# Three moves in the order of work: first loads on a second queue, chains that end in the next stage, vectors put behind a norm

## The chip, the cores and the metric

The kernel runs on one core of a Trainium2 chip. The core has a matrix engine (TensorE, PE in the profile; its weight loads are PEld), VectorE (DVE), ScalarE (ACT), GpSimd (POOL), SyncE (SP, which here only issues DMAs), and 16 DMA engines. The metric is the device time of one execution in microseconds (us). Three timed runs of the kernel before gave 2895.5, 2902.23 and 2908.86 us; the median is 2902.23 us.

## What is computed

The input is a sequence `x` of 512 rows by 1024 columns and a context of 256 rows. All is float32. Cut to what matters:

```
first_block:
  mod = silu(c) @ w_ada + b_ada                 # six vectors of 1024, likewise from c_ctx
  h   = rms_norm(x, gain) * (1 + scale) + shift # and the same for ctx
  q, k, v, gates of 4 retention and 4 mLSTM heads = h @ w_in
  retention and mLSTM scans, forward and backward, started from the context's states
  x += g1 * ((sig(.)*(y_ret @ w_ret_up) + sig(.)*(y_ml @ w_ml_up)) @ w_out)
  x += g2 * swiglu(norm(x));  x = rms_norm(x, final_gain)
second_block, four layers (latent attention, sliding window, long convolution, latent attention):
  mx = silu(c_2) @ w_mod[layer] + b_mod[layer]  # three vectors of 1024, likewise from c_ctx_2
  hx = rmsnorm(x, g_pre) * (1 + scale) + shift  # and the same for ctx
  x += gate * rmsnorm(mixer(hx, hc), g_post)
```

## The kernel before, in words

**Products.** Activations lie with features on partitions, `x` as 8 tiles of 128x512, the context as 8 of 128x256. A float32 matrix is split into a high and a low part (`split`, L398 on ScalarE and L399 on VectorE), and a product is three matmuls per 128 rows of weights (`mac`, L442 to L444). A weight tile is loaded by SP into one of 4 buffers `raw` (`wload`, L404), split, and used.

**Order.** The code is written as Python generators; each `yield` ends a step. `weave((g, n), (h, m), ...)` always takes the next step of the generator that is furthest behind its number n, and so merges them; a generator with more steps than its number goes on alone at the end. `islice(g, n)` hands over n steps, `chain` puts generators one behind another. The order so written is a priority: a planner walks it with modelled durations, takes for each engine the earliest-written instruction that is ready and whose tile is free, and fixes each engine's order from that. Each engine then runs its list in order. Tiles come from pools: `big` has 53 buffers of 128x512 (tag b), `tmp` 10, `P` 8, the PSUM pools 4 banks and 2 pairs of banks.

**Start** (`first_block`, from L604). SP issues in this order: the constants (L294), 8 small rows of vectors (`rows`, L340), 8 small loads of the filter network (`filter_setup`, L1827 to L1838), 8 loads of `x` and 4 of the context (`load_T`, L485, 256 KB each), then the modulation weights. `load_T` transposes what landed (L491), squares are summed (L232, L236), and `norm1` scales (L571 to L577).

**Vectors.** `mod_stream` makes 18 vectors, 6 of `w_ada` and 12 of `w_mod`; each takes 4 steps (`mod`), each step 2 loads of 512 KB and 16 narrow matmuls (L505), gathered on VectorE (L508, L510) and transposed at the end (L514). `self.mods(n)` weaves in n steps; `need(i)` runs the stream until vector i is there.

**First block's heads.** `dense(pair, ml)` has 12 steps (ND): two for keys, one for the context's keys, two for values, one for the context's values, two for states `S` (L839, L840), and four for queries and gates. `ret_chain(pair)` has 20 steps, 10 for each of 2 heads, and is woven by the number NR = 16; `ml_chain(pair)` has 34 (NM), 17 a head: 4 for the queries, 8 for the four key blocks, 2 for denominators (L1010 to L1015), 2 that spread them and scale (`over_columns` L1386, L1019, L1020), and 1 for the sum (L1024, L1025). Each stage weaves the dense work of one pair with the chain of the pair before and 4 vector steps; the fifth weaves 10 gate products (`bgate`) with the last chain. Chains take their tiles from `tmp` and `P`, dense steps from `big`.

**First latent layer.** `norm3(1)`, the last norm of the first block for the second half of the sequence, is kept as `self.pending` and runs inside the layer's first 41 steps (`stream_tiles`, `lead`): 24 of the norm woven with 6 of products on what is ready, then 8 and 3 steps for the second half. 22 steps with 11 weight tiles follow. In `mla` (L1549) the whole is woven as `(tiles, 30)` with `self.mods(12)`. The fourth layer calls the same code when the stream has nothing left; there the pending norm is `rest` of the third layer.

Of the kernel before, what the change touches and what calls it, by code (L numbers as in the profile page):

```python
# [19 lines left out]
N = 512  # L20
NC = 256
# [10 lines left out]
NR = 16  # L32
NM = 34
# [5 lines left out]
ND = 12  # L39
NM1 = 34  # L40
# [36 lines left out]
WB = 3  # L77
# [115 lines left out]
def weave(*items):  # L193
    for _ in mix(*items):
        pass
# [8 lines left out]
def chain(*gens):  # L204
    for g in gens:
        yield from g
# [49 lines left out]
class Kern:  # L256
# [347 lines left out]
    def first_block(self):  # L604
        nc, I = self.nc, self.I
        st = ExitStack()
        c1 = mp = self.pool("c1", 1, st=st)
        C, X = self.actf(KT, NC), self.actf(KT, N)
        first = self.rows(False, nc.sync)
        next(first)  # L610
        setup = self.filter_setup()
        next(setup)
        inputs = [self.load_T(I["x"][0], N, X), self.load_T(I["ctx"][0], NC, C)]
        for g in inputs:
            next(g)
        self.second_setup()
        late = self.rows(True, nc.gpsimd)
        next(late)
# [286 lines left out]
        def ret_chain(pair):  # L905
            o = out[pair, False]
            for u in range(2):
                h = 2 * pair + u

                strips = [self.P(), self.P()]  # L910
                dist = self.t(), self.t()
                of = self.coff["first"]["dist"][0]
                for z in range(2):
                    nc.sync.dma_start(dist[z], I["k_first"][:, of + 384 * z:of + 384 * z + 512])
                nc.vector.tensor_scalar(strips[0][:, 0:384], dist[0][:, 0:384], lg[:, 4 + h:5 + h], -1.0, ALU.mult, ALU.mult)
                nc.vector.tensor_scalar(strips[1][:, 128:512], dist[1][:, 128:512], lg[:, h:h + 1], None, ALU.mult)
                tmp = self.t(128)
                m0, m1 = strips[0][:, 384:512], strips[1][:, 0:128]
                nc.vector.tensor_scalar(tmp, dist[1][:, 0:128], 0.0, lg[:, 4 + h:5 + h], ALU.min, ALU.mult)
                nc.vector.tensor_scalar(m0, dist[1][:, 0:128], 0.0, lg[:, h:h + 1], ALU.max, ALU.mult)  # L920
                nc.vector.tensor_tensor(m0, m0, tmp, ALU.subtract)
                nc.scalar.activation(strips[0], strips[0], AF.Exp)
                nc.scalar.activation(strips[1][:, 128:512], strips[1][:, 128:512], AF.Exp)
                nc.vector.tensor_tensor(m0, m0, self.ident, ALU.add)
                nc.vector.tensor_copy(m1, m0)
                yield
                S = yield from scores(o.K[u], o.q[u])
                acc = self.mm()
                for d in range(2):
                    qd = HL(self.P(dt=F32R), self.P(dt=F32R))  # L930
                    g = self.t()
                    nc.scalar.activation(g, cf["tpos"] if d == 0 else cf["tpos"][:, ::-1], AF.Exp, scale=lg[:, 4 * d + h:4 * d + h + 1])
                    nc.vector.tensor_tensor(g, g, o.q32[u], ALU.mult)
                    self.split(qd, g)
                    self.mac(acc, [(o.S[u][d], qd)], start=d == 0, stop=False)
                    (finish if d else roots)()
                    yield
                for i in range(4):
                    P = self.t()
                    a = 384 - 128 * i  # L940
                    n0 = 512 - a
                    nc.vector.tensor_tensor(P[:, 0:n0], S[i][:, 0:n0], strips[0][:, a:512], ALU.mult)
                    if n0 < 512:
                        nc.vector.tensor_tensor(P[:, n0:512], S[i][:, n0:512], strips[1][:, 128:128 + 512 - n0], ALU.mult)
                    Ph = HL(self.t(dt=F32R), self.t(dt=F32R))
                    self.split(Ph, P)
                    self.mac(acc, [(o.V[i][:, 128 * u:128 * u + 128], Ph)], start=False, stop=i == 3)
                    yield
                o32 = self.t()
                nc.scalar.copy(o32, acc)  # L950
                nc.vector.tensor_tensor(o.g[u], o.g[u], o32, ALU.mult)
                tail.append((self.rstd1(o32, 4), o.g[u], o.g[u]))
                yret32[h] = o.g[u]
                yield
# [77 lines left out]
        def bgate(k):  # L1032
            for off in (4112, 5136):
                t = sg[k, off] = self.b()
                nc.scalar.activation(t, self.proj(self.wm(W, 0, KT, off + 128 * k), hx, N), AF.Tanh, scale=0.5)
                yield

        weave((dense(0, False), ND), (chain(idle(GD), gates()), 10 + GD), (units, UC))
        weave((dense(1, False), ND), (ret_chain(0), NR), self.mods(4))
        weave((dense(0, True), ND), (ret_chain(1), NR), self.mods(4))  # L1040
        weave((dense(1, True), ND), (ml_chain(0), NM), self.mods(4))
        nbg = 5
        weave((chain(*(bgate(k) for k in range(nbg))), 2 * nbg), (ml_chain(1), NM1), self.mods(4))
        yret, yml = self.acts(4, N), self.acts(4, N)
        for k in range(4):
            self.split(yret[k], yret32[k])
# [32 lines left out]
        w1, s1 = [], [b, b, b, P, P, None, None, None]  # L1079
        weave((merge(), 22), self.mods(4), (chain(idle(PA), self.ahead(I["w_out"][0], 0, KT, s1, w1)), PA + PE0 + PZ))  # L1080
        X = self.actf(KT, N)
# [83 lines left out]
        w2, s2 = [], [b, P, P, P, P, None, None, None]  # L1165
# [308 lines left out]
    def mla(self, j, ctx_out, bg, end):  # L1474
        nc, I = self.nc, self.I
# [60 lines left out]
        def tiles(cs, lag, last=False):  # L1536
            for _ in self.stream_tiles([(load(c), use(c, 0), use(c, 1) if ctx_out or c in (4, 5, 6) else None) for c in cs], lag):
                for x in list(due):
                    if x[0]:
                        x[0] -= 1  # L1540
                    elif next(x[1], None) is None:
                        due.remove(x)
                yield
            while due and last:
                for x in list(due):
                    if next(x[1], None) is None:
                        due.remove(x)

        weave((tiles(order, WB - 2, True), 30), bg)  # L1549

        H = {}

# [265 lines left out]
        return chain(attend(units[-LT:]), stageB(*units[-1])), 10 * LT + 5  # L1818


    def filter_setup(self):

        nc, I = self.nc, self.I
        cp = self.c2
        sm = cp.tile([64, 8], F32, name="fsm")
        w1 = cp.tile([33, 64], F32, name="fw1")
        nc.sync.dma_start(w1, I["c_f_w1_2"][0])  # L1827
        zs = []
        for n, kz in ((N, "k_fz"), (NC, "k_fzc")):
            z = self.t(n)[0:33, :]  # L1830
            nc.sync.dma_start(z, I[kz])
            zs.append(z)
        for i, nm in enumerate(("c_f_b1_2", "c_f_b2_2", "c_f_freq_2")):
            nc.sync.dma_start(sm[:, i:i + 1], I[nm].rearrange("a (f o) -> (a f) o", o=1))
        w2 = cp.tile([64, 64], F32, name="fw2")
        nc.sync.dma_start(w2, I["c_f_w2_2"][0])
        self.ftc = cp.tile([128, 6], F32, name="ftc")
        nc.sync.dma_start(self.ftc, I["k_ftime"])  # L1838
        yield
        for i in range(2):  # L1840
            nc.vector.tensor_tensor(sm[:, 3 + i:4 + i], sm[:, i:i + 1], sm[:, 2:3], ALU.mult)
        self.fh = []

        def sine(ps, n, b):
            arg, r = self.t(n)[0:64, :], self.t(n)[0:64, :]
            nc.scalar.activation(arg, ps, AF.Identity, scale=sm[:, 2:3], bias=b)
            nc.vector.tensor_scalar(r, arg, float(1 / (2 * math.pi)), MAGIC, ALU.mult, ALU.add)
            nc.vector.tensor_scalar(r, r, -MAGIC, None, ALU.add)
            nc.vector.scalar_tensor_tensor(arg, r, -TP1, arg, ALU.mult, ALU.add)
            nc.vector.scalar_tensor_tensor(arg, r, -TP2, arg, ALU.mult, ALU.add)  # L1850
            nc.vector.tensor_scalar(arg, arg, 3.1415925, -3.1415925, ALU.min, ALU.max)
            nc.scalar.activation(arg, arg, AF.Sin)
            return arg

        for z, n in zip(zs, (N, NC)):
            ps = self.mm()
            nc.tensor.matmul(ps[0:64, :n], w1, z, start=True, stop=True)
            h = sine(ps[0:64, :n], n, sm[:, 3:4])
            yield
            ps = self.mm()  # L1860
            nc.tensor.matmul(ps[0:64, :n], w2, h, start=True, stop=True)
            h = sine(ps[0:64, :n], n, sm[:, 4:5])
            f = self.b(dt=F32R)[:, :n]
            nc.scalar.copy(f[0:64, :], h)
            nc.vector.tensor_tensor(f[64:128, :], h, f[0:64, :].bitcast(F32), ALU.subtract)
            self.fh.append(f)
            yield
# [284 lines left out]
```

## Time and profile before

| | before |
|---|---|
| timed runs, median | 2902.23 us |
| profiled execution, its own time | 2904.86 us |
| its span, first to last instruction | 2903.1 us |
| PE busy | 2771.4 us, 95% |
| DVE, ACT, POOL busy | 1800.1, 1321.4, 131.7 us |
| mean granted TensorE clock | 0.981 |
| DMA | 318.95 MB, 110 GB/s over the span |

All times of the trace count from the first instruction of the profiled execution. Busy is time in which an engine ran an instruction; the share of the whole says little of a stage, so the rows further down are of stretches. A wait names what ended it. The granted clock is 1.00 at TensorE's upper level (2.4 GHz) and 0.50 at the lower (1.2 GHz).

### The profile page before, as it was taken

To read this page: it belongs to the slowest core of one execution; us is meant where nothing else is said; L and a number is where in the kernel's file an instruction comes from. 1 tells how busy PE (TensorE), PEld (TensorE's weight loads), DVE (VectorE), ACT (ScalarE), POOL (GpSimd) and SP (SyncE) were. 2 spreads that over 40 slices of the span, in tenths; PEclk is the share of its full clock that TensorE was granted. 3 is DMA by queue.
4 is the path that set the end of the run, shared out by engine and by line. 5 is a ranking of instruction groups with operands and counts; after the bars stand their busy time and mean duration, and the time that the engine had idled before them with its cause. 6 is when DMAs were issued, how large, how long until landed. Compare 5 with 4: busy or idle time off the path is not lost. (4 is left out here: it accounts for less than half of the span.)

```text
span 2903.1 us, 43841 instructions
## 1 busy us (share of the span) xinstructions
PE 2771.4 (95%) x17106; PEld 2370.5 (82%) x17106; DVE 1800.1 (62%) x3599; ACT 1321.4 (46%) x2538; POOL 131.7 (5%) x166
## 2 busy tenths in 40 slices
PE   6999999999999999999999999989999998999998
PEld 4888878888777787888889877878988886887887
DVE  6665455555655556246767577788576667744674
ACT  4344344336556333345555565665332223544553
POOL 1000000000000000000000000000021212000000
PEclk8999999999999999999999999999999999999998
DMA  7234232544555537311234241124122226431122
GB/s 265 81 116 124 73 102 80 161 143 158 169 164 176 167 102 240 88 59 46 77 105 137 74 118 46 45 59 131 62 82 84 84 84 193 135 94 61 59 80 70
DMA packets 365827, 318.95 MB, mean 110 GB/s; under 512 B 17511, under 2 KB 326517, under 8 KB 365620
## 3 DMA queue, kind: packets, MB, share of 16 engines
q1 hardware_dynamic: 365204, 315.99, 35.4%
q8 instruction: 134, 2.20, 0.3%
q14 instruction: 73, 0.60, 0.1%
q0 software_dynamic: 416, 0.17, 0.0%
HBM read 273.90 MB, written 42.21 MB: 109 GB/s over the span
## 5 line engine op out<-in xcount | busy, mean ns | idle before, releaser
L442 PE MATMUL mm<-b,whi 128*128 128x512 f32 (+1 forms) x2548 | 897.2, 353 | 5.9 <-ACT whi L398 2.6
L444 PE MATMUL mm<-b,wlo 128*128 128x512 f32 (+1 forms) x2548 | 888.7, 349 | 0.9 <-DVE wlo L399 0.9
L443 PE MATMUL mm<-b,whi 128*128 128x512 f32 (+1 forms) x2548 | 888.8, 349 | 0.0
L442 PEld LDWEIGHTS mm<-b,whi 128*128 128x128 f32 x2548 | 487.7, 192 | 71.6 <-ACT whi L398 4.1
L444 PEld LDWEIGHTS mm<-b,wlo 128*128 128x128 f32 x2548 | 487.3, 191 | 61.4 <-DVE wlo L399 1.9
L443 PEld LDWEIGHTS mm<-b,whi 128*128 128x128 f32 x2548 | 488.2, 192 | 59.5 <-issue 0.5
L399 DVE TENSOR_TENSOR wlo<-raw,whi 128x1024 fp32r<-128x1024 f32 (+3 forms) x286 | 292.1, 1024 | 244.3 <-ACT whi L398 228.1
L398 ACT CAST whi<-raw 128x1024 fp32r<-128x1024 f32 (+3 forms) x286 | 252.4, 885 | 390.9 <-PE mm L443 247.9
L1402 ACT ACTIVATE P<-mm,sm 128x768 f32<-128x768 f32 (+3 forms) x176 | 128.0, 728 | 139.0 <-DVE sm L1399 66.9
L444 PE MATMUL mm<-b 128*128 128x256 f32 (+1 forms) x628 | 189.6, 302 | 0.5 <-DVE b L399 0.3
L442 PE MATMUL mm<-b,P 128*128 128x256 f32 x560 | 162.5, 290 | 4.1 <-ACT b L576 3.1
L1397 DVE TENSOR_REDUCE sm<-mm 128x1 f32<-128x768 f32 (+3 forms) x176 | 128.6, 734 | 60.9 <-PE mm L1620 30.4
L442 PE MATMUL mm<-b 128*128 128x256 f32 (+1 forms) x500 | 158.2, 318 | 8.0 <-ACT P L1402 4.3
L443 PE MATMUL mm<-b,P 128*128 128x256 f32 x560 | 160.7, 287 | 0.9 <-DVE b L577 0.6
L399 DVE TENSOR_TENSOR t<-mm,t 128x512 fp32r<-128x512 f32 (+1 forms) x208 | 136.8, 665 | 28.9 <-ACT t L398 27.4
L443 PE MATMUL mm<-b 128*128 128x256 f32 (+1 forms) x500 | 153.1, 307 | 0.3 <-DVE b L399 0.3
L398 ACT CAST t<-mm 128x512 fp32r<-128x512 f32 (+1 forms) x208 | 116.0, 570 | 53.0 <-PE mm L1416 48.7
L246 POOL TENSOR_TENSOR rs<-rs,mhalf 128x2 f32<-128x2 f32 (+1 forms) x44 | 41.3, 939 | 2137.5 <-DVE rs L245 1991.0
L236 DVE TENSOR_TENSOR t<-t 128x256 f32<-128x256 f32 (+1 forms) x216 | 92.6, 441 | 73.0 <-ACT t L232 70.4
L232 ACT ACTIVATE t<-b 128x256 f32<-128x256 f32 (+1 forms) x252 | 100.5, 431 | 70.4 <-DVE b L1102 42.4
L1416 PE MATMUL mm<-ct,P 128*128 128x128 f32 x768 | 122.4, 277 | 9.9 <-ACT P L1402 6.0
L444 PEld LDWEIGHTS mm<-b 128*128 128x128 f32 x628 | 120.5, 192 | 5.8 <-DVE b L399 1.3
(343 smaller groups left out, 5081.1 us busy)
## 6 DMA issues: line engine op xcount, KB each, us to landing
raw<-in_w_mod_dram SPq DMA_DIRECT2D x96, 512.0 KB, 3.9
raw<-in_w_ada_dram SPq DMA_DIRECT2D x48, 512.0 KB, 3.8
raw<-in_w_in_dram SPq DMA_DIRECT2D x48, 512.0 KB, 4.1
raw<-in_w_ffn_in_dram SPq DMA_DIRECT2D x44, 512.0 KB, 3.9
raw<-in_c_w_in_dram SPq DMA_DIRECT2D x32, 512.0 KB, 4.5
raw<-in_a_w_in_dram SPq DMA_DIRECT2D x28, 512.0 KB, 4.2
ks<-t SPq DMA_DIRECT2D x48, 256.0 KB, 3.4
raw<-ks SPq DMA_DIRECT2D x24, 512.0 KB, 3.2
```

The lines of the kernel that those rows point to most:

```text
L232: self.k.nc.scalar.activation(sq, x, AF.Square)
L236: self.k.nc.vector.tensor_tensor(self.acc, self.acc, sq, ALU.add)
L246: nc.gpsimd.tensor_tensor(s[:, 4:4 + nt], s[:, :nt], self.k.mhalf[:, :nt], ALU.pow)
L398: self.nc.scalar.copy(dst.hi, src)
L399: self.nc.vector.tensor_tensor(dst.lo, src, dst.hi.bitcast(F32), ALU.subtract)
L442: nc.tensor.matmul(ps, l.hi, r.hi, start=start and i == 0, stop=False)
L443: nc.tensor.matmul(ps, l.hi, r.lo, start=False, stop=False)
L444: nc.tensor.matmul(ps, l.lo, r.hi, start=False, stop=stop and i == n - 1)
L1397: nc.vector.tensor_reduce(top[:, j:j + 1], S, AX.X, ALU.max)
L1402: nc.scalar.activation(P, S, AF.Exp, bias=b, scale=scale, accum_out=sums[:, j:j + 1])
L1416: self.nc.tensor.transpose(ps[:, 128 * i:128 * i + 128], b, self.ident)
```

## The change

Three edits. At the start, `x` and the context are issued on SP straight behind the constants, and the 8 rows and 8 filter loads are issued on ScalarE's queue. In the first block, each chain hands over its steps short of the end (13 of the retention chain's, 31 of the mLSTM chain's), and the rest is chained ahead of the next stage's chain. In `mla`, the first 36 steps are woven alone and the vectors with what follows.

```
-        first = self.rows(False, nc.sync)
+        inputs = [self.load_T(I["x"][0], N, X), self.load_T(I["ctx"][0], NC, C)]
+        first = self.rows(False, nc.scalar)
         next(first)
-        setup = self.filter_setup()
-        next(setup)
-        inputs = [self.load_T(I["x"][0], N, X), self.load_T(I["ctx"][0], NC, C)]
         for g in inputs:
             next(g)
+        setup = self.filter_setup(nc.scalar)
+        next(setup)
...
-        weave((dense(1, False), ND), (ret_chain(0), NR), self.mods(4))
-        weave((dense(0, True), ND), (ret_chain(1), NR), self.mods(4))
-        weave((dense(1, True), ND), (ml_chain(0), NM), self.mods(4))
+        c = 3
+        ret, ml = [ret_chain(0), ret_chain(1)], [ml_chain(0), ml_chain(1)]
+        weave((dense(1, False), ND), (islice(ret[0], NR - c), NR - c), self.mods(4))
+        weave((dense(0, True), ND), (chain(ret[0], islice(ret[1], NR - c)), NR), self.mods(4))
+        weave((dense(1, True), ND), (chain(ret[1], islice(ml[0], NM - c)), NM), self.mods(4))
         nbg = 5
-        weave((chain(*(bgate(k) for k in range(nbg))), 2 * nbg), (ml_chain(1), NM1), self.mods(4))
+        weave((chain(*(bgate(k) for k in range(nbg))), 2 * nbg), (chain(ml[0], ml[1]), NM1 + c), self.mods(4))
...
-        weave((tiles(order, WB - 2, True), 30), bg)
+        ts = tiles(order, WB - 2, True)
+        n = 16 + 6 + 8 + 3 + 3
+        weave((islice(ts, n), n))
+        weave((ts, 24), bg)
...
-    def filter_setup(self):
+    def filter_setup(self, dma):
...
-        nc.sync.dma_start(w1, I["c_f_w1_2"][0])
+        dma.dma_start(w1, I["c_f_w1_2"][0])
...
```

## Rows read from the trace of the kernel before

**Rows 1.** the page, part 1: busy us, share of the span, instructions

```profile
PE 2771.4 (95%) x17106; PEld 2370.5 (82%) x17106; DVE 1800.1 (62%) x3599; ACT 1321.4 (46%) x2538; POOL 131.7 (5%) x166
```

**Rows 2.** timeline of SP, 0 to 130 us: start, length, instruction, count

```profile
1.17 0.36 SPq L340 DMA_DIRECT2D rows<-in_c_dram  x1
...
7.60 0.59 SPq L1838 DMA_DIRECT2D ftc<-in_k_ftime_dram  x1
8.23 3.75 SPq L485 DMA_DIRECT2D b<-in_x_dram  x8
12.03 3.93 SPq L485 DMA_DIRECT2D b<-in_ctx_dram  x4
16.27 25.68 SPq L404 DMA_DIRECT2D raw<-in_w_ada_dram  x16
```

**Rows 3.** windows, start: length, busy of PE PEld DVE ACT POOL, clock, DMA share, GB/s

```profile
0.00:8.20 8.20, 0.43 (x1) 0.18 (x1) 4.94 (x33) 2.79 (x4) 7.18 (x18) 1.00 0.33 63
...
16.30:24.30 8.00, 7.83 (x41) 4.93 (x41) 4.47 (x9) 5.17 (x10) 0.00 (x0) 1.00 1.03 405
24.30:48.30 24.00, 16.60 (x141) 7.42 (x140) 16.68 (x43) 10.01 (x25) 1.04 (x1) 0.77 0.87 298
48.30:68.00 19.70, 17.03 (x75) 11.28 (x75) 15.99 (x32) 9.61 (x13) 0.70 (x1) 0.67 1.00 320
```

**Rows 4.** waits of PE, 0 to 60 us: total, times, longest

```profile
PE mm L491 <- DMA b<-in_x_dram: 6.0, 2, 4.8
PE mm L505 <- DMA raw<-in_w_ada_dram: 4.2, 6, 1.1
PE mm L505 <- ACT t L1846: 2.9, 1, 2.9
```

**Rows 5.** timeline of PE, 333 to 352 us

```profile
336.80 0.50 PE L442 MATMUL mm<-t,b 128*128 128x512 f32 x1 [1.01 <-ACT t L398]
...
350.54 0.68 PE L840 MATMUL mm<-b,t 128*128 128x128 f32 x4 [3.19 <-DVE t L839]
```

**Rows 6.** timeline of DVE, 328 to 358 us

```profile
348.05 0.69 DVE L1020 TENSOR_TENSOR t<-mm,t 128x512 f32<-128x512 f32 x1 [0.23 <-ACT t L1019]
...
349.50 0.69 DVE L1025 SCALAR_TENSOR_TENSOR t<-b,t 128x512 f32<-128x512 f32 x1
350.11 0.87 DVE L839 TENSOR_SCALAR t<-b,cwk 128x128 f32<-128x128 f32 x4
```

**Rows 7.** windows in the first block's heads

```profile
200.00:270.00 70.00, 70.00 (x452) 59.47 (x451) 39.54 (x80) 29.38 (x47) 1.01 (x1) 1.00 0.35 106
...
347.00:351.30 4.30, 1.11 (x11) 0.90 (x9) 3.68 (x8) 1.65 (x3) 0.00 (x0) 1.00 0.42 122
351.30:358.20 6.90, 6.90 (x34) 4.60 (x34) 2.95 (x6) 1.64 (x4) 0.00 (x0) 0.51 0.08 13
```

**Rows 8.** one step of a retention chain, DVE by form, 140 to 300 us

```profile
L399 DVE TENSOR_TENSOR t<-t 128x512 fp32r<-128x512 f32 x16 | 11.1, 691 | 8.8 <-ACT t L398 7.0 <-PE mm L443 1.8
...
L942 DVE TENSOR_TENSOR t<-mm,P 128x512 f32<-128x512 f32 x4 | 2.7, 686 | 0.2 <-PE mm L443 0.2
```

**Rows 9.** windows around the leads of the first and fourth layer

```profile
1118.00:1156.00 38.00, 33.00 (x304) 22.31 (x297) 16.66 (x52) 8.31 (x20) 1.39 (x2) 0.96 0.89 296
1136.40:1139.80 3.40, 3.40 (x22) 2.41 (x18) 0.00 (x0) 0.00 (x0) 0.00 (x0) 0.50 1.01 390
1156.00:1260.00 104.00, 104.00 (x616) 92.44 (x615) 35.13 (x52) 38.18 (x66) 3.66 (x3) 1.00 0.32 93
2541.00:2566.00 25.00, 23.15 (x187) 22.39 (x188) 18.05 (x48) 8.87 (x24) 2.09 (x3) 1.00 0.21 69
```

**Rows 10.** waits of PE, 1118 to 1156 us

```profile
PE mm L505 <- DMA raw<-in_w_mod_dram: 2.8, 3, 1.1
```

**Rows 11.** timeline of PE, 300 to 380 us: one vector step

```profile
328.25 1.07 PE L505 MATMUL mm<-raw,condc 128*32 128x256 f32 x16
```

**Rows 12.** the page, part 6: a vector load, KB, us to landing

```profile
raw<-in_w_mod_dram SPq DMA_DIRECT2D x96, 512.0 KB, 3.9
```

More of the change, by code (lines that the diff above doesn't have):

```diff
@@ L1830, in filter_setup @@
             z = self.t(n)[0:33, :]
-            nc.sync.dma_start(z, I[kz])
+            dma.dma_start(z, I[kz])
             zs.append(z)
         for i, nm in enumerate(("c_f_b1_2", "c_f_b2_2", "c_f_freq_2")):
-            nc.sync.dma_start(sm[:, i:i + 1], I[nm].rearrange("a (f o) -> (a f) o", o=1))
+            dma.dma_start(sm[:, i:i + 1], I[nm].rearrange("a (f o) -> (a f) o", o=1))
         w2 = cp.tile([64, 64], F32, name="fw2")
-        nc.sync.dma_start(w2, I["c_f_w2_2"][0])
+        dma.dma_start(w2, I["c_f_w2_2"][0])
         self.ftc = cp.tile([128, 6], F32, name="ftc")
-        nc.sync.dma_start(self.ftc, I["k_ftime"])
+        dma.dma_start(self.ftc, I["k_ftime"])
         yield
```

## The prediction

> **What bounds the kernel now.** I read the busy times first. PE is busy 2771.4 us, and DVE, the next, 1800.1 [rows 1]: the kernel ends when PE's list ends. The profiled execution took 2904.86 us, of which the span is 2903.1 and 1.76 lie around it. Time can be won only where PE stands idle, where its clock is at the lower level, or where its work waits in a start that is not yet PE's. So I read the windows and PE's waits in the three places that the edits touch, and not the shares of the whole. The reader should see three different limits there.
>
> At the start the limit is data. PE first waits 6.0 us for `x`, and then six times, 4.2 us together, for loads of `w_ada` [rows 4]. In the first 8.2 us the DMA engines move 63 GB/s, then 405, 298 and 320 GB/s until 68 us [rows 3]. They are almost empty at first and hardly stop afterwards. SP explains it: from 1.17 us it issues 16 small loads, the last at 7.60 us, and the first load of `x` goes out at 8.23 us, the first of `w_ada` at 16.27 [rows 2].
>
> In the heads PE is full, 70.00 of 70.00 us in the third stage, with one hole: of 4.30 us from 347 PE works 1.11, and the next 6.90 us run at granted clock 0.51, the lower of its two levels (1.2 GHz) [rows 7].
>
> In the first latent layer's lead PE is idle 5.0 of 38 us and the DMA engines move 296 GB/s; the same code in the fourth layer, with no vectors beside it, has 1.85 us idle in 25 [rows 9]. Of the 5.0 us, 2.8 are waits of L505 for `w_mod` [rows 10].
>
> **The change, part by part.**
>
> *Start.* SP loses 16 issues that stand ahead of `x`: 8.23 - 1.17 = 7.06 us [rows 2]. The same 16 go to ACT, in front of everything that ACT does. Their length on ACT is not in the trace; on SP they took 0.29 to 0.6 us each, 7 us in all. ACT has 2.79 us of work in the first 8.2 us [rows 3], so it would be free near 10 us. What waits behind them are the conditions for the first L505 and half of the copies behind `x`'s transposes. Today `x` goes out at 8.23 us and ctx at 12.03 [rows 2]; moved, `x`'s last pieces land about when ACT comes free. I charge 1 us for that. What `x` moves past on SP needs nothing earlier than before; the rows go out at the same time as today on the other queue, and the filter loads follow them, with no load of `x` in front on ACT. Everything behind is paced by bytes or by DVE (16.0 of 19.7 us busy while the norm is applied [rows 3]), so it shifts as a whole. The bounds: at best the whole 7.06 us, at worst 3 us lost, if each issue takes about twice as long on ACT (14 us and 2.79 of work, against the 10 I allow) and half of the 7 us more reaches the copies. I take 6 us gained, near the upper end, because the row of the first 8.2 us shows the engines idle.
>
> Against it stands the Trainium skill, page "DMA: Bandwidth & Descriptors", section "Issuing engines are not separate DMA queues": DMAs from several engines run on the same 16 DMA engines, and spreading them saves only issue time. By that rule nothing is gained in bandwidth, and the gain cannot exceed the issue time removed, which is the bound of 7.06 us. Where the trace shows 298 to 405 GB/s the rule bites, and at 63 GB/s it does not.
>
> *Heads.* The work is the same; only its place moves. Written out, the merge puts seven retention steps of each pair (20 less 13) into the next stage, and three mLSTM steps. The boundary of the second and third stage lies in 200 to 270 us and shows nothing to win: PE has no idle there [rows 7], since the planner already fills the chain's last steps with the next stage's products; I take the boundary behind it to be alike. The hole at 347 is what counts. It is not at a boundary: it is the end of the first mLSTM head in the fourth stage. In the old merge the states step comes right behind the sum: DVE does the scaling (L1020) at 348.05, the sum (L1025) at 349.50, and only then L839, for which L840 waits 3.19 us [rows 5, 6]. Seven retention steps now come ahead in that stage, the states steps fall before the denominators, and behind the scaling come a query's products (24 matmuls), which need nothing of the chain. So the wait goes, 3.19 us, and with it the stretch at 0.51: 6.90 us that would take half, 3.4 us. The earlier wait of 1.01 us for a split [rows 5] may go or stay. What is late next is the denominators' chain itself, with only a states step in front of it; I charge 1 us. Gain 3.2 + 3.4 - 1.0 = 5.6, taken as 5.5. The bounds: 7.6 us gained (3.2 + 3.4 + 1.0), or 6.6 lost, a second hole of that size with the first one still there.
>
> *Latent layer.* Twelve vector steps leave the lead: 24 loads of 512 KB [rows 12] and 12 times 1.07 us of PE [rows 11]. Those 12.8 us of PE are paid again later, so they count nothing. What counts is the idle beside them. Without them the lead should look as in the fourth layer: 1.85 us idle instead of 5.0 [rows 9], 3.15 gained. The stretch at 0.50 from 1136.4 lasts 3.4 us [rows 9], and 1.7 of it is lost; it follows the waits for `w_mod`, so it goes too. Sum 4.85, taken as 5. What ends last then is the norm's chain, and the fourth layer shows what that costs; its chain has one DVE step more per tile than `norm3`, so it is no easier case. The new place has 22 steps with 11 weight tiles. PE is busy 104.00 of 104 us there and the DMA engines move 93 GB/s [rows 9]. 24 x 0.52 = 12.6 MB more in 104 + 13 = 117 us is 108 GB/s more, 200 in all, half of the 405 of [rows 3]; a load lands in 3.9 us [rows 12], and in 3.9 us a step pair of about 10 us asks for three of four buffers. So I charge no wait. The bounds: 7 us gained (half steps of L505 becoming whole), or 3 lost, if the 2.8 us of waits move along and the norm alone idles 3 more than now. In the fourth layer the stream is spent (44 steps in the first block, 12 + 8 + 8 in the layers, 72 of 72), so the second call of the same code changes nothing.
>
> **Sum.** 6 + 5.5 + 5 = 16.5 us: 2904.86 - 16.5 = 2888.4 for a profiled execution. The profiled one lay 2.6 us above the median of 2902.23, so the median should be 2902.2 - 16.5 = 2885.7, taken as **2886 us**. All three at their upper ends give 7.1 + 7.6 + 7.0 = 21.7, which is 2880.5; all three at their lower ends give 12.6 us lost, 2914.8.
>
> **The rivals.**
>
> *One gain does not come* (2891 to 2892). The likeliest is the vectors' waits moving with them: they are 4 loads per pair of tiles at worst, SP issues in order, and L505 stands in PE's list ahead of products that are ready. For it: L505 is the instruction that waits for DMA wherever it is dense. Against: in 200 to 270 us vector steps run beside dense weights at 106 GB/s with PE never idle [rows 7]. Or ACT's issues cost what SP's did, or a new hole replaces that at 347. Price: 5 to 6 us of the 16.5.
>
> *Two gains do not come*, the change then does little of what it says: 2897.
>
> *The chains lag and the pool `big` runs out* (slower). A pair holds keys 4, values 4, states 2 or 4, queries 6 and gates 2 tiles; the inputs hold 24, tables and filter parts about 6. Counting by the code, the old merge asks for up to 59 of 53 tiles in the third stage, the new one for up to 63, since the older pair lives seven steps longer. Dense steps then wait for tiles, and PE has only the chain, where a step shows L942 (0.69) and L399 (0.69) [rows 8] with a cast on ACT between them that I take as long: 2 us a step without cover, an estimate. 7 + 7 + 3 = 17 steps would cost 34 us; less the 11 us of the other two edits it is 2902.2 + 23 = 2925. It decides if the shortage holds back whole products and not just their last steps. Against: at 59 of 53 PE is full now [rows 7], because the chain's ready steps are taken first, which simply undoes part of the edit. A mild form, 8 of the 17 steps, gives 16 - 11 = 5 us slower, 2907.
>
> **How the numbers follow.** The forecast as a whole 0.50, one gain missing 0.30, two missing 0.12, slower 0.08. Half a percent of 2902.2 is 14.5 us, about what a measurement of this kernel can tell from no change: faster means below 2887.7, slower above 2916.7. The forecast at 2886 lies close to that bound; with the bounds of its terms and medians that scatter by several us, I give it 0.75 below, one missing 0.3, two missing 0.1: 0.375 + 0.09 + 0.01, 0.48. Slower by over half a percent 0.04, the rest 0.48. The range runs from 2873, the upper ends with the scatter of the runs shown (6.7 us either way), to 2902, which leaves out the slower rival and part of the two missing.
>
> **What would show it.** SP issues `x` at about 1.2 us and `w_ada` near 9; the first window's GB/s rises, and all that follows comes some 6 us sooner. No wait of L840 near the first mLSTM head's end and the granted clock 1.00 through the fourth stage. No L505 among PE's waits in the lead and few in the 22 steps behind. Wrong would be: PE idle between retention steps in the third and fourth stage, ACT's first copy behind `x` later than its transposes by several us, or L505 waiting for `w_mod` in the new place.

## The result, and the profile after

| | before | after |
|---|---|---|
| timed runs, median | 2903.89 us (4 runs) | 2935.32 us (4 runs, 2930.68 to 2941.95) |
| ratio of the times | | 1.0113, 95% interval 1.0096 to 1.0130 |
| profiled execution, its span | 2903.1 us | 2928.9 us |
| mean granted clock | 0.981 | 0.977 |

The change made the kernel 31 us slower; 2886 us was forecast, with 2902 as the upper end. The busy times hardly move. From the page of the kernel after, part 1:

```profile
PE 2781.9 (95%) x17106; PEld 2373.6 (81%) x17106; DVE 1798.9 (61%) x3599; ACT 1325.3 (45%) x2539; POOL 131.4 (4%) x166
```

Against [rows 1] PE has the same 17106 matmuls and 10.5 us more busy time. The spans differ by 25.8 us, so the larger part of that is idle time. Both kernels have the same matmuls in nearly the same order, so I matched them by their number in PE's list and took the difference of their starts, in us (one execution of each kernel):

| matmul number (its start before) | after | start alone | heads alone | lead alone |
|---|---|---|---|---|
| 600 (119 us) | +2.2 | +4.3 | +0.4 | +0.8 |
| 1200 (222 us) | +3.7 | +7.1 | +3.1 | +1.5 |
| 1800 (316 us) | +23.7 | +7.1 | +23.3 | +1.5 |
| 2400 (423 us) | +37.4 | +6.9 | +37.2 | +1.2 |
| 6000 (1105 us) | +37.6 | +7.1 | +37.5 | -4.0 |
| 7200 (1289 us) | +30.8 | +7.0 | +38.0 | -10.8 |

So in the kernel after, the start costs 2 us, the heads between 119 and 423 us cost 35, and the lead gives 6.8 back: between numbers 6000 and 7200 all of the moved vector matmuls run in every one of these kernels. Single executions scatter. The lead alone, which changes nothing before 1105 us, drifts by 5 us between numbers 2400 and 6000, and the start's +2.2 in one execution and +4.3 in the other are no measure finer than that.

**The start after.** SP's timeline, and ACT's behind it, of the kernel after (columns as in [rows 2]):

```profile
1.18 8.98 SPq L485 DMA_DIRECT2D b<-in_x_dram  x8
...
14.57 1.78 SPq L404 DMA_DIRECT2D raw<-in_w_ada_dram  x4
16.46 7.54 SPq L646 DMA_DIRECT2D xd<-b  x7
...
31.27 13.88 SPq L404 DMA_DIRECT2D raw<-in_w_ada_dram  x10
```

```profile
0.74 0.63 ACTq L1832 DMA_DIRECT2D fw<-in_c_f_w_dram  x1
...
13.03 0.36 ACTq L1843 DMA_DIRECT2D ftc<-in_k_ftime_dram  x1
13.42 1.28 ACT L355 ACT_TABLE_LOAD   x1 [13.42 <-DMA b<-in_ctx_dram]
...
18.82 1.28 ACT L591 ACT_TABLE_LOAD   x1
...
20.82 1.28 ACT L1857 ACT_TABLE_LOAD   x1
22.11 0.63 ACT L1857 ACTIVATE t<-t 64x512 f32<-64x512 f32 x1
```

`x` is issued at 1.18 us as intended, but its 8 issues now stretch over 8.98 us instead of 3.75 [rows 2], so `w_ada` starts at 14.57, only 1.7 us before the old 16.27 and not 7. The issues themselves are no longer than before: one takes 0.33 to 0.43 us, against 0.42 to 0.44. Between them SP waits. Its waits in the first 16 us, first before, then after:

```profile
SPq L485 <- DMA b<-in_x_dram: 1.6, 1, 1.6
```

```profile
SPq L485 <- DMA b<-in_x_dram: 5.0, 4, 3.6
SPq L485 <- DMA t<-in_k_fzc_dram: 1.1, 1, 1.1
SPq L485 <- DMA fsm<-in_c_f_b_dram: 0.8, 1, 0.8
...
SPq L485 <- DMA rows<-in_c_dram: 0.7, 1, 0.7
```

What SP waits for is that earlier loads land, those that ACT issued among them; with two smaller waits it is 8.4 us for `x` and the context. The trace names a semaphore (the counter that tells of a landing) for every load: the loads and stores of SP and ACT share eight of them, and an issue waits until what had its semaphore before has landed. So the program has at most eight of these under way, whichever engine issues them. Before, the eight in front of `x` were small ones, and `x`'s issues found them landed; now the small loads and the 256 KB pieces of `x` take turns, and ACT's issues are held as SP's are. ACT's 16 last until 13.4 us, though the issues alone make up 6.2 us of that (6.4 on SP before).

The last of the rows therefore goes out at 6.42 us instead of 3.62. In PE's list a matmul on the rows (L346) stands ahead of `x`'s transposes (L491), and [rows 4] leave out that PE waited for it before as well. Before, then after:

```profile
6.02 0.43 PE L346 MATMUL mm<-ct,rows 104*128 104x104 f32 x1 [6.02 <-DMA rows<-in_final_gain_dram]
```

```profile
10.24 0.41 PE L346 MATMUL mm<-ct,rows 104*128 104x104 f32 x1 [10.24 <-DMA t<-in_k_fz_dram]
```

So the first transpose comes at 10.44 us against 11.23, though the first load of `x` went out 7.05 us earlier.

On SP, 7 stores of `x` (L646) go out ahead of most of `w_ada`. ACT's first table loads, which the kernel before did at 0.73 to 9.99 us, come behind its 16 issues, in among the filter network's sine. PE's list shows who waits for that. First PE of the kernel before, which had no such wait, then of the kernel after:

```profile
21.43 1.07 PE L1861 MATMUL mm<-t,fw 64*64 64x512 f32 x2
...
23.37 0.64 PE L505 MATMUL mm<-raw,condc 128*32 128x256 f32 x8
```

```profile
22.80 1.96 PE L1866 MATMUL mm<-t,fw 64*64 64x512 f32 x2 [3.74 <-ACT t L1857]
...
26.35 1.93 PE L505 MATMUL mm<-raw,condc 128*32 128x256 f32 x16
```

The filter's second matmul (L1866, the old L1861) waits 3.74 us for the sine (L1857, the old L1852). The first vector step L505 stands behind it in the list and starts at 26.35 us instead of 23.37.

**The heads after.** Three rows of PE's timeline, and ACT around the middle one:

```profile
214.08 0.50 PE L442 MATMUL mm<-P,b 128*128 128x512 f32 x1 [2.67 <-ACT P L398]
...
262.53 1.22 PE L840 MATMUL mm<-b,t 128*128 128x128 f32 x4 [7.61 <-ACT b L793]
...
391.13 1.09 PE L1388 MATMUL mm<-ct,den 128*128 128x128 f32 x4 [2.99 <-DVE den L1015]
```

```profile
254.73 0.59 ACT L793 COPY b<-mm 128x512 f32<-128x512 f32 x1 [2.91 <-PE mm L443]
255.22 1.08 ACT L398 CAST b<-mm 128x512 fp32r<-128x512 f32 x2
256.17 0.74 ACT L932 ACTIVATE t<-b,lg 128x512 f32<-128x512 f32 x1
259.04 0.62 ACT L398 CAST P<-t 128x512 fp32r<-128x512 f32 x1 [2.12 <-DVE t L933]
260.41 0.72 ACT L932 ACTIVATE t<-b,lg 128x512 f32<-128x512 f32 x1 [0.76 <-DVE P L399]
261.89 0.59 ACT L793 COPY b<-mm 128x512 f32<-128x512 f32 x1 [0.76 <-DVE t L933]
```

The hole of [rows 5] is gone, but new ones stand at 211, 255 and 388 us. In the longest, PE stands still for 7.61 us for a copy of L793 (the context's keys and values) into a tile of `big`, while ACT and DVE do single steps of the handed-over chain (L932, L933, L398) between the two copies. Behind each hole the clock is lower. Windows of the kernel after (columns as in [rows 3]):

```profile
200.00:225.00 25.00, 22.32 (x109) 17.40 (x108) 11.43 (x19) 6.46 (x10) 1.38 (x1) 0.93 0.27 84
...
250.00:275.00 25.00, 17.39 (x90) 14.52 (x89) 13.41 (x28) 9.44 (x16) 0.00 (x0) 0.73 0.23 64
...
375.00:400.00 25.00, 21.14 (x93) 15.88 (x93) 11.01 (x28) 6.09 (x13) 0.00 (x0) 0.71 0.23 63
sum 200.00, PE 177.39 PEld 146.32 DVE 85.57 ACT 62.95 POOL 5.16; mean PE 22.17 PEld 18.29 DVE 10.70 ACT 7.87 POOL 0.65
```

and the sum of the same eight windows before:

```profile
sum 200.00, PE 195.24 PEld 163.86 DVE 104.92 ACT 80.67 POOL 4.41; mean PE 24.40 PEld 20.48 DVE 13.11 ACT 10.08 POOL 0.55
```

PE is busy 17.9 us less in these 200 us, and idle so much more. Busy time multiplied by what the clock lacks, summed over the eight windows, is about 16 us after and 3.5 before. Together that is about 30 us of the 35, roughly, as the two kernels do not hold quite the same work between 200 and 400 us.

**The lead after.** Where [rows 10] has L505 waiting for `w_mod`, PE's waits of the kernel after in 1105 to 1200 us are these alone:

```profile
PE mm L1388 <- POOL rs L246: 3.1, 3, 1.5
PE mm L243 <- DVE t L236: 0.4, 1, 0.4
```

L505 is not among them. What is left are waits for the norm itself (L246).

### The profile page after: what moved, and what is told of

Its sections match the earlier page's. It is cut to its first block, busy times and chain, and to the rows that moved or that the text cites. A ratio compares the mean times of both kernels' runs of the same rounds, so it can differ in the third digit from the quotient of the medians.

```text
span 2928.9 us, 43842 instructions
## 1 busy us (share of the span) xinstructions
PE 2781.9 (95%) x17106; PEld 2373.6 (81%) x17106; DVE 1798.9 (61%) x3599; ACT 1325.3 (45%) x2539; POOL 131.4 (4%) x166
## 5 line engine op out<-in xcount | busy, mean ns | idle before, releaser
L442 PE MATMUL mm<-b,whi 128*128 128x512 f32 (+1 forms) x2548 | 896.7, 352 | 6.7 <-ACT whi L398 2.7
L442 PEld LDWEIGHTS mm<-b,whi 128*128 128x128 f32 x2548 | 485.9, 191 | 76.1 <-issue 5.2
L398 ACT CAST whi<-raw 128x1024 fp32r<-128x1024 f32 (+3 forms) x286 | 253.1, 888 | 426.5 <-PE mm L443 270.4
L442 PE MATMUL mm<-b 128*128 128x256 f32 (+1 forms) x500 | 158.0, 318 | 8.0 <-ACT P L1404 4.3
L442 PE MATMUL mm<-b,P 128*128 128x256 f32 x560 | 161.8, 289 | 3.4 <-ACT b L576 2.8
L398 ACT CAST t<-mm 128x512 fp32r<-128x512 f32 (+1 forms) x208 | 116.1, 570 | 51.2 <-PE mm L1418 47.7
L246 POOL TENSOR_TENSOR rs<-rs,mhalf 128x2 f32<-128x2 f32 (+1 forms) x44 | 41.2, 937 | 2163.0 <-DVE rs L245 2163.0
```

Source lines behind the costliest of these rows:

```text
L246: nc.gpsimd.tensor_tensor(s[:, 4:4 + nt], s[:, :nt], self.k.mhalf[:, :nt], ALU.pow)
L398: self.nc.scalar.copy(dst.hi, src)
L442: nc.tensor.matmul(ps, l.hi, r.hi, start=start and i == 0, stop=False)
```

## The experiments

Each was compared with the kernel before on the same chip. Theory at the outset: the heads lose by the pool `big`, and the start by what the later rows and filter loads hold up; the rivals are the written-out order and the early stores of `x`.

**Each edit alone: start, heads, lead.** The diffs are the three parts of the change shown above.

> Only the start's edit. Theory: ScalarE's 16 issues, drawn out to 13.4 us beside the loads of x in the changed kernel, hold back the copies and the sine on which TensorE's list waits, so the first key rotation (L783) comes about 2 us later than before and the whole is 2 us slower (0 to 5). Rival, the prediction's own: the start gains and the loss seen at 77 us in the changed kernel came from the other edits' effect on the planned order; then 4 to 7 us faster.

> Only the hand-over of the chains' last steps. Theory: nearly the whole loss is here, the pool of 53 tiles runs short while two pairs live side by side; 30 to 40 us slower, with TensorE waiting 2 to 8 us at a time between 200 and 400 us. Rival: the three edits only hurt together, through the planned order; then within 10 us of before.

> Only the vectors behind the pending norm. Theory: as predicted, 5 us faster (between 2 and 12), no wait of L505 for w_mod in the lead. Rival: the waits move with the vectors, no change (within 2 us).

| | time | ratio, 95% interval |
|---|---|---|
| start alone | 2905.29 us | 1.0018, 1.0005 to 1.0031 |
| heads alone | 2940.10 us | 1.0129, 1.0108 to 1.0149 |
| lead alone | 2893.68 us | 0.9976, 0.9966 to 0.9987 |

Against 2901.11 us these are +4, +39 and -7 us; their sum, +36, is about the 31 of the whole change. By its interval the start costs between 1.5 and 9 us. All three forecasts held. The heads alone show the same holes as the kernel after, 7.6 us at L840 among them. For the lead, here is the stretch from matmul 6000 to 7200, first before, then with the lead alone:

```profile
1104.90:1288.80 183.90, 176.89 (x1203) 149.46 (x1202) 76.35 (x158) 65.42 (x127) 5.75 (x6) 0.99 0.44 139
```

```profile
1100.90:1278.00 177.10, 173.45 (x1203) 148.46 (x1202) 76.43 (x158) 65.67 (x127) 4.80 (x6) 1.00 0.46 145
```

The same matmuls take 6.8 us less: PE is idle 3.4 us less and busy 3.4 us less, of which 1.7 are the stretch at 0.50 [rows 9], now at full clock. In the new place PE does not wait:

```profile
1150.00:1260.00 110.00, 110.00 (x723) 92.29 (x722) 33.48 (x61) 32.30 (x58) 2.71 (x3) 1.00 0.50 156
```

The lead alone is faster than before and after, and the best version of this study.

**Heads with the pool relieved, and its control.** Eight tiles come free if the context's keys and values are taken from the first 256 rows of `x`; the starting states then miss the context, and the instructions stay the same in kind and number. Once with the heads' edit, once on the kernel before.

```
-                self.proj_t(hc, 128 * s, w, ps[:, 256 * s:256 * s + 256])
+                self.proj_t(hx, 128 * s, w, ps[:, 256 * s:256 * s + 256])
```

> The hand-over of the chains' last steps, and the context's keys and values are computed from the first 256 rows of x instead of the context (same products, the retention and mLSTM start states are left without the context), so that the context's 8 tiles of the pool of 53 come free after the first stage. Theory of the pool: demand falls from 63 to 55 and most of the loss goes, at most 8 us slower than before, or faster. Rival, the written order itself exposes the chains' steps: still 25 to 40 us slower.

> The kernel before, with the context's keys and values computed from the first 256 rows of x (the start states are left without the context), so that 8 tiles of the pool of 53 come free after the first stage and the old order asks for at most 51. It is the control of e4_heads_free. If the pool did not hold the old order back: no change, within 4 us. If it did (it asks for 59 of 53): up to 10 us faster, and the difference of 18.7 us between e4_heads_free and before understates what the written order costs by as much.

**Heads with a later cut, with and without the relief.** The retention chains hand over 5 steps instead of 7.

```
-        weave((dense(1, False), ND), (islice(ret[0], NR - c), NR - c), self.mods(4))
-        weave((dense(0, True), ND), (chain(ret[0], islice(ret[1], NR - c)), NR), self.mods(4))
+        weave((dense(1, False), ND), (islice(ret[0], 15), 15), self.mods(4))
+        weave((dense(0, True), ND), (chain(ret[0], islice(ret[1], 15)), NR), self.mods(4))
```

> As e4_heads_free (context left out of the start states, 8 tiles free), but a retention chain hands over its last 5 steps and not 7, so that the next stage doesn't begin with the scaled queries (L932, L933). If what is left of the loss in e4_heads_free comes from where the written order puts the chains' steps: its two holes of 2.9 us before a product with the scaled queries go, with the clock's fall behind them, and it is 5 to 10 us faster than e4_heads_free (2910 to 2915). Rival, it is still the pool, now 55 of 53: no faster than e4_heads_free by more than 3 us.

> The edit of the heads alone, but with 5 steps of each retention chain handed over (the cut behind step 15) and no tiles of the pool freed. With 8 tiles freed the same cut was 6.7 us slower than its control. Pool theory (the demand by count is 63 tiles of 53, as with the 7 steps): 20 us or more slower than the kernel before, with TensorE's wait of several us at L840 <- L793 still there. Order theory (what counts is where the chain is cut): under 10 us slower, that wait gone.

| retention steps handed over | pool as it is | 8 tiles freed |
|---|---|---|
| none | 1 | 0.9990 (0.9976 to 1.0004) |
| 5 | 1.0111 (1.0089 to 1.0132) | 1.0027 (1.0011 to 1.0044) |
| 7 | 1.0129 (1.0108 to 1.0149) | 1.0065 (1.0047 to 1.0084) |

The relief does nothing measurable where nothing is handed over, and gives 19 to 24 us where something is. With 5 steps it cures most of the loss (32 us to 8), with 7 about half (37 to 19), which is neither the at most 8 of the pool theory nor the 25 to 40 of its rival. With 5 steps and the tiles freed the kernel is 9 us slower than its control by the medians, not the 6.7 that the last expectation names. PE's waits in 190 to 400 us, first with 5 steps handed over, then with 5 steps and the tiles freed:

```profile
PE mm L840 <- ACT b L793: 6.4, 1, 6.4
...
PE mm L442 <- ACT P L398: 4.3, 1, 4.3
...
```

```profile
PE mm L442 <- ACT P L398: 4.7, 1, 4.7
PE mm L442 <- ACT t L398: 2.0, 2, 1.2
PE mm L1388 <- DVE den L1015: 1.6, 1, 1.6
...
```

L840's wait for the copy is gone with the tiles freed, and so it is the shortage that made it, by way of the order that the planner fixed. What stays is the wait at the place where the handed-over chain takes up: its first scaled query (L442 <- P) stands in PE's list right behind the last product of the stage, and its split is 4.7 us late. The waits with 7 steps and the tiles freed:

```profile
PE mm L442 <- ACT P L398: 5.9, 2, 2.9
PE mm L1388 <- DVE den L1015: 3.0, 1, 3.0
...
PE mm L840 <- ACT b L793: 1.3, 1, 1.3
```

Here the late queries come at both retention hand-overs, and the denominators wait. So both theories hold in part: with 7 steps the pool is about half of the loss, and with the tiles freed the later cut is another 11 us. What makes the last 8 is not separated: by count 55 of 53 tiles are still asked for, and a late query is still there. Neither a larger pool `big` nor the chains' own pools `tmp` and `P` were varied.

**Start, filter loads behind `x` on SP.** Nothing on ACT; rows, `x`, context, filter in this order on SP.

```
-        setup = self.filter_setup()
-        next(setup)
         inputs = [self.load_T(I["x"][0], N, X), self.load_T(I["ctx"][0], NC, C)]
...
+        setup = self.filter_setup()
+        next(setup)
```

> Rows, x, context and then the filter loads, all on SP: x is issued near 3.9 us and ScalarE's queue issues nothing. Theory that ScalarE's issues cost the start its gain: 2 to 4 us faster than before, the copies behind x no longer wait for ScalarE until 14 us. Rival, the stores of x (L646), which in e1_start stand ahead of the loads of w_ada on SP from 17.8 us: they move ahead here too and the first vectors are no earlier than before; 0 to 5 us slower.

It took 2911.60 us, 1.0029 (1.0015 to 1.0043). From its SP timeline:

```profile
3.98 3.70 SPq L485 DMA_DIRECT2D b<-in_x_dram  x8
...
16.89 1.85 SPq L404 DMA_DIRECT2D raw<-in_w_ada_dram  x4
```

and of PE:

```profile
16.93 1.94 PE L1857 MATMUL mm<-t,fw 33*64 33x512 f32 x2 [3.53 <-DMA t<-in_k_fz_dram]
...
26.92 1.96 PE L1861 MATMUL mm<-t,fw 64*64 64x512 f32 x2 [2.62 <-ACT t L1852]
```

By the ratio that is about 8 us slower, more than either theory said, and the rival's sign is there: the stores of `x` go ahead of most of `w_ada` here too. The 8 loads of `x` are issued in 3.70 us, since only small loads, which had landed, stood in front of them. But the filter loads and `w_ada` behind now wait for `x` and the context to land, and `w_ada` starts at 16.89 us, later than the old 16.27. So ACT is not needed for a loss: with eight loads under way at most, a load that is moved ahead holds back those behind, and late filter loads delay the sine and the vectors.

**Start, the stores of `x` held back.** A copy of one column into itself makes each store wait for the norm's use of its tile.

```
-                (nc.gpsimd if QS else nc.sync).dma_start(self.xd[k], X[k])
+                nc.vector.tensor_copy(X[k][:, 0:1], X[k][:, 0:1])
+                nc.sync.dma_start(self.xd[k], X[k])
```

> The start's edit, and a copy of one column of each tile of x onto itself behind the norm, so that the 8 stores of x can't go ahead of the loads of w_ada. Rival (the stores cost the start its gain): 4 to 8 us faster than e1_start's ratio of 1.0018, that is 0 to 4 us faster than before. Theory of ScalarE's issues: as e1_start, 3 to 6 us slower than before.

2908.85 us, 1.0012 (0.9994 to 1.0030). `w_ada` is no longer interrupted:

```profile
14.40 31.53 SPq L404 DMA_DIRECT2D raw<-in_w_ada_dram  x16
```

but the second vector comes at 53.9 us, against 55.5 with the start alone and 50.7 before. In the kernel after, where the stores do go ahead, it comes at 53.7. So holding the stores back shows no gain at the vector. The time is 3 us above before, near the forecast of the theory of ScalarE's issues, but its interval reaches into both forecasts.

**Start, the filter's steps out of the way, and a control.** The counts of filter steps placed ahead of the vectors and in the first norm are set to 0, with and without the start's edit.

```
-U0 = 2
-U1 = 2
+U0 = 0
+U1 = 0
...
-UB = 100
+UB = 0
```

> The edit of the start, and the three counts U0, U1, UB at 0, so that the filter network's steps leave the list ahead of the first vector and run beside the first dense stage. Theory (with the rows and filter loads later, the filter's matmuls, which stand ahead of the first vector in TensorE's list, wait for ScalarE's sines, and the vectors wait behind them): the waits of the matmuls at the filter's lines go, the second vector is out at or before the 50.7 us of the kernel before (55.4 with the edit of the start alone), and the time is 4 to 8 us under that of the edit of the start alone. Rival (w_ada's arrival sets the vectors): the second vector stays at 53 to 55 us and the time within 2 us of the edit alone.

> Control: the kernel before with U0, U1, UB at 0 alone. If the filter's place in TensorE's list costs something in the kernel before too, the second vector comes 1 to 3 us earlier than 50.7 and the time falls by as much; if w_ada's arrival sets the vectors there, it stays within 1 us, and the first dense stage, which now holds the filter's steps, may give 2 us back the other way.

2915.56 us (1.0051, 1.0033 to 1.0069) with the edit, 2917.12 (1.0053, 1.0035 to 1.0071) without. The writes of the first two vectors (first and last start) in the start alone, then here with the edit and without it:

```profile
L519 DVE TENSOR_TENSOR mv<-mm,pc x4: 154/160/167, 41.2 to 55.5; 128x8 f32<-128x8 f32 x4
```

```profile
L519 DVE TENSOR_TENSOR mv<-mm,pc x4: 155/161/167, 34.5 to 47.8; 128x8 f32<-128x8 f32 x4
```

```profile
L519 DVE TENSOR_TENSOR mv<-mm,pc x4: 156/162/167, 35.0 to 48.2; 128x8 f32<-128x8 f32 x4
```

The second vector comes 7.7 us earlier than with the edit alone, which shows that the filter's matmuls in PE's list held it. Without the edit it comes 2.5 us earlier than before. The forecast of 4 to 8 us for the whole fell all the same: one filter matmul now waits 11.7 us in the first dense stage, with the edit (shown) and without, and at matmul 600 both kernels are some 15 us behind.

```profile
75.97 1.97 PE L1861 MATMUL mm<-t,fw 64*64 64x512 f32 x2 [11.70 <-ACT t L1852]
```

**The same, spread over the norm, with the lead.** `UB = 4` instead of 0.

> The lead of the latent layer, and the filter network's four steps spread over the 16 steps of the first norm (U0 = U1 = 0, UB = 4), without the edit of the start. With UB = 0 the second vector came at 48.2 us against 50.7, but one wait of 11.7 us for the sines came behind it. Theory: spread over the norm, the sines end under the norm's own work, the second vector stays near 48 us, and the time is 1 to 3 us under that of the lead alone (2893.7). Rival: ScalarE and VectorE, which set the norm's pace, carry the sines there, the norm's steps become 3 to 6 us longer, and the time is no better than the lead alone.

> The same with the edit of the start. Theory (the edit of the start loses only through the filter's matmuls that stand ahead of the vectors): with these behind the vectors it costs nothing, second vector at 47 to 48.5 us, time within 2 us of the same kernel without it. Rival (the later rows and the drawn-out issues cost something by themselves): second vector 2 us later or more, and the time 3 us or more above.

2912.76 us without the start's edit (1.0040, 1.0023 to 1.0057), 2912.14 with it (1.0046, 1.0029 to 1.0063). The filter's two waits are 6.7 and 7.5 us in both, so the rival holds, and costs more than it said: 19 us against the lead alone, not 3 to 6. The sine's steps on DVE take turns there with the norm's. With the filter behind the vectors, the start's edit costs nothing measurable, and gains nothing either: the second vector is at 50.3 us with it, 49.6 without. In the eight kernels whose start is the old one it lies between 50.7 and 52.2, so a difference of 0.7 says nothing.

**The lead with the mLSTM hand-over alone.** Retention as before; the first mLSTM chain hands 3 steps to the gates' stage.

```
+        c = 3
+        ml = [ml_chain(0), ml_chain(1)]
-        weave((dense(1, True), ND), (ml_chain(0), NM), self.mods(4))
+        weave((dense(1, True), ND), (islice(ml[0], NM - c), NM - c), self.mods(4))
...
-        weave((chain(*(bgate(k) for k in range(nbg))), 2 * nbg), (ml_chain(1), NM1), self.mods(4))
+        weave((chain(*(bgate(k) for k in range(nbg))), 2 * nbg), (chain(ml[0], ml[1]), NM1 + c), self.mods(4))
```

> The lead of the latent layer, and of the heads only the hand-over of 3 steps of the first mLSTM chain into the gates' stage; both retention chains end in their own stage as before. If the mLSTM hand-over is worth what the forecast gave it (1 to 2 us), 8 to 9 us faster than before, against 7.4 for the lead alone; if it too runs into waits for tiles or late operands, 2 to 5 us faster only, and TensorE shows waits of 2 to 3 us at the lines of the mLSTM chain behind the third dense stage.

2898.99 us, 0.9989 (0.9976 to 1.0001), against 0.9976 for the lead alone; the intervals overlap. In the trace the part between matmuls 1800 and 2400 is 2.7 us shorter than before, the wait of [rows 5] falls from 3.19 to 1.0, and the lead gives 6.0 us. So the mLSTM hand-over by itself makes no new hole there, and the loss of the heads belongs to the retention chains' hand-overs or to both together. Why the gain does not show in the median stays open, and the version is not better than the lead alone.

## Why the prediction was wrong

**Start: 6 us gained was forecast, about 4 were lost** (2 in the trace of the whole change). Three steps failed. "SP loses 16 issues that stand ahead of `x`" was read as 7.06 us for everything behind. It brought 7 us to the first load of `x`, but 1.7 us to `w_ada`. The wait that the prediction put at nothing is that of an issue for an earlier load to land: on SP 1.6 us among `x` and the context before, 8.4 after. "The rows go out at the same time as today" failed by the same wait: their last load left 2.8 us later, L346 started 4.2 us later, and `x`'s transposes behind it gained 0.8 us. And "the filter loads follow them", at no charge, left out who waits for them: the sine, by way of the filter's second matmul ahead of the first L505 in PE's list. So what stands behind the first load of `x` does not "shift as a whole". The bound of "twice as long on ACT" came near the 12.7 us by luck: the issues took no longer there, they were held. And the prediction's "PE first waits 6.0 us for `x`" passed over the wait for the rows ahead of it. With the filter moved away, the edit gains only 0.4 us at the second vector, inside the scatter. By the rule of the Trainium skill's page "DMA: Bandwidth & Descriptors", section "Issuing engines are not separate DMA queues", the issue time was the most that could be gained; the trace agrees, with 1.7 of 7.06 us left at `w_ada`.

**Heads: 5.5 us gained was forecast, 35 to 37 were lost.** The rival "the chains lag and the pool `big` runs out" came true in part, with a chance of 0.08. Its price of 34 us was near by luck: it was 17 steps of 2 us each, while the trace has a few long waits with a lower clock behind them, and the pool makes 19 to 24 us of the loss. The step that failed is the argument against it: "at 59 of 53 PE is full now, because the chain's ready steps are taken first, which simply undoes part of the edit". A demand of 59 by count does no harm before, as the control with freed tiles shows (0.9990), but that was no evidence for 63: the products of the next pair did wait, 7.61 us at L840 for a copy into `big`, and that wait falls to 1.3 us with eight tiles freed. The second step that failed is "I take the boundary behind it to be alike": an idle-free boundary [rows 7] showed that there was nothing to win, and I did not ask what the edit would put there. The late scaled query at the hand-over, 2.67 to 4.72 us with a lower clock behind it, is such a new wait. The one about L840 <- L839 held: that wait went. "I charge 1 us" for the denominators was too little; they wait 2.99 us and the clock falls behind them.

**Lead: 5 us gained was forecast, 7.4 came** (6.8 in the matched matmuls). Its mechanism was right: no L505 among the waits, full clock, no waits in the new place. Its two terms were right too: 3.15 us of idle time against 3.4 measured, and 1.7 of clock. What the sum left out is that PE is busy another 1.7 us less for the same matmuls; the upper bound of 7 us had named a source for it, half steps of L505 becoming whole, but no run separates that.

## What to carry to other kernels

Before moving a chain's tail into the next stage, count what it keeps alive there: a pool that is overdrawn on paper without loss says nothing of four tiles more, and relieving the pool by a stand-in, with a control, shows at once whether it is the cause. Before moving small loads out of the way, follow each to the instruction that waits for it, and look for what stands behind that instruction in the engine's own list. Count too how many loads the program lets be under way: where issues wait for landings, a second issuing engine takes turns with the first. Weigh each edit alone: here one of three was worth having.

## What the runs showed of the hardware

An issue took as long from ACT as from SP: 16 small ones 6.2 us in all on ACT after, 6.4 on SP before, and a load of `x` 0.33 to 0.43 us with ACT issuing beside it, 0.36 to 0.44 without. What stretched them, to 12.7 us on ACT and 8.98 on SP, were the program's own waits for earlier loads to land.
